# RMS norm with repeated rows: stores and later loads issued by GpSimd in place of SyncE

## The chip, the cores and the metric

The kernel runs on one core of one Trainium2 chip. The metric is the device time of one execution in microseconds (us), the median over several runs. Profiles come from one execution each.

## The reference

```python
def reference(x, gamma):            # x: 8 x 512 x 2048 float32, gamma: 2048 float32
    x_rep = np.repeat(x, 2, axis=1) # each row twice: 8 x 1024 x 2048
    rms = np.sqrt((x_rep ** 2).mean(axis=-1, keepdims=True) + 1e-6)
    x_norm = x_rep / rms
    return (x_norm * gamma[None, None, :]).astype(np.float32)
```

Each of the 4096 rows is divided by its root mean square, multiplied by gamma, and written twice. The input has 33.6 MB, the output 67.1 MB.

## The kernel before

The 4096 rows are handled in four loads of 1024 rows. A load (`load`, L49) brings 8 rows of 2048 floats to each of 128 partitions, 64 KB in a partition, 8.39 MB in all. Each load gives two stores (`store`, L52) of the same size, since every row goes out twice; a store takes 8 finished rows (4 rows, each repeated) of each partition. So there are four loads and eight stores, twelve transfers of 8.39 MB. The 64 KB of a partition are one contiguous run in memory and in the buffer.

All rows live in one buffer `y` of 24 rows per partition, seen as three regions of 8 rows: `first`, `second` and `third`. Function `four` handles two loads, `n` and `m`, and is called twice, for loads 0 and 1 and then for loads 3 and 2. Load `n` goes to the last half of `first` and the first half of `second` (`first + K`), load `m` to `third`. From there:

- `squares` (ACT, L63 and L67) sums the squares of each row and takes the root.
- `scale` (DVE, L76 and L77) takes the reciprocal and multiplies the row by it and by gamma, into the place where the first copy of the row stands in the output.
- `repeat` (L84) copies each finished row to the place beside it, on ACT in five of the seven calls of one `four`, on DVE in two (one in each half of load `n`).
- `store` sends a region out.

The order is written out by hand (`manual_schedule`): each engine runs its instructions in the order of the program text, and the semaphores are put in by the framework. The stores of one `four` are, in order: `n`'s first half out of `first`, `n`'s second half out of `second`, `m`'s first half out of `first`, `m`'s second half out of `third`. The region `first` is written again (L77) when its earlier store has landed. The loads of the second `four` wait for stores of the first: load 3 overwrites parts of `first` and `second`, so it waits for the first three stores; load 2 overwrites `third` and waits for the fourth.

Before the change all twelve transfers are issued by SyncE, so they stand in one queue in the order load, load, four stores, load, load, four stores. Gamma is loaded by four small transfers issued by ACT, ahead of the second load in the program text, and spread over the partitions by two GpSimd instructions (L133, L137).

Of the kernel before, what the change touches and what calls it, by code (L numbers as in the profile page):

```python
# [1 line left out]

# [4 lines left out]


@with_exitstack
def kernel(  # L10
    ctx: ExitStack,
    tc: tile.TileContext,
    x: bass.AP,
    gamma: bass.AP,
    out: bass.AP,
):
    nc = tc.nc
    P = nc.NUM_PARTITIONS
    f32 = mybir.dt.float32
    Act = mybir.ActivationFunctionType  # L20
    Alu = mybir.AluOpType

    B, S, D = x.shape
    Bo, So, Do = out.shape
    R = So // S
    assert R == 2 and D == Do and B == Bo and So == S * R
    eps = 1e-6
    inv_d = 1.0 / float(D)


    K = 4
    N = B * S
    ntiles = N // (P * K)
    assert N % (P * K) == 0 and ntiles == 8
    H = 2
    x_t = x.rearrange("b s d -> (b s) d").rearrange("(n p k) d -> n p k d", p=P, k=H * K)
    out_t = out.rearrange("b s d -> (b s) d").rearrange("(n p h j) d -> n h p (j d)", p=P, h=H, j=K * R)

    singles = ctx.enter_context(tc.tile_pool(name="singles", bufs=1))
    rows = ctx.enter_context(tc.tile_pool(name="rows", bufs=1))  # L40
    junk = ctx.enter_context(tc.tile_pool(name="junk", bufs=1, space=bass.MemoryType.PSUM))
    small = ctx.enter_context(tc.tile_pool(name="small", bufs=4))

    y = rows.tile([P, 3 * K * R, D], f32, name="y")
    first, second, third = 0, K * R, 2 * K * R

    def load(n, at):  # L49
        nc.sync.dma_start(out=y[:, at : at + H * K, :], in_=x_t[n])  # L50

    def store(n, h, to):  # L52
        nc.sync.dma_start(
            out=out_t[n, h], in_=y[:, to : to + K * R, :].rearrange("p j d -> p (j d)")
        )

    def squares(at, rows):

        n = len(rows)
        ss = small.tile([P, n], f32, name=f"ss{n}")  # L60
        for c, k in enumerate(rows):
            sq = junk.tile([P, D], f32, name="sq")
            nc.scalar.activation(  # L63
                out=sq[:], in_=y[:, at + k, :], func=Act.Square, accum_out=ss[:, c : c + 1]
            )
        rms = small.tile([P, n], f32, name=f"rms{n}")
        nc.scalar.activation(out=rms[:], in_=ss[:], func=Act.Sqrt, scale=inv_d, bias=eps_t[:])  # L67
        return rms

    def scale(at, to, rows, rms, at_once=K):  # L70
        n = len(rows)
        rstd = small.tile([P, n], f32, name=f"rstd{n}")
        for c, k in enumerate(rows):
            if c % at_once == 0:
                part = slice(c, min(c + at_once, n))
                nc.vector.reciprocal(out=rstd[:, part], in_=rms[:, part])  # L76
            nc.vector.scalar_tensor_tensor(  # L77
                out=y[:, to + R * k, :], in0=y[:, at + k, :], scalar=rstd[:, c : c + 1],
                in1=gamma_b[:], op0=Alu.mult, op1=Alu.mult,
            )  # L80

    def repeat(to, k0, k1, copy):
        y_r = y[:, to + R * k0 : to + R * k1, :].rearrange("p (k r) d -> p k r d", r=R)
        copy(out=y_r[:, :, 1, :], in_=y_r[:, :, 0, :])  # L84

    ctx.enter_context(tc.manual_schedule())

    half = K // 2
    up, down = list(range(K)), list(range(K - 1, -1, -1))

    def four(n, m, constants, at_once):


        load(n, first + K)
        constants()
        load(m, third)
        for rows, n_at_once in ((up[:half], half), (up[half:], at_once)):
            scale(first + K, first, rows, squares(first + K, rows), n_at_once)
        repeat(first, 0, half, nc.scalar.copy)
        repeat(first, half, K, nc.vector.tensor_copy)  # L100
        store(n, 0, first)
        scale(second, second, down, squares(second, down))
        repeat(second, half, K, nc.scalar.copy)
        repeat(second, 0, half, nc.vector.tensor_copy)
        store(n, 1, second)
        roots = [squares(third + h * K, up) for h in range(H)]
        scale(third, first, up, roots[0])
        repeat(first, 0, half, nc.scalar.copy)
        repeat(first, half, K, nc.scalar.copy)
        store(m, 0, first)  # L110
        scale(third + K, third, up, roots[1])
        repeat(third, 0, K, nc.scalar.copy)
        store(m, 1, third)

    gamma_b = singles.tile([P, D], f32, name="gamma_b")
    G, E = 16, 3
    C = D // G - E
    gamma_s = y[0:1, 0:2, :].rearrange("p k (c d) -> p (k c) d", c=G // 2)
    gamma_t = y[0:1, 2, :]
    eps_t = singles.tile([P, 1], f32, name="eps_t")  # L120

    def constants():
        nc.scalar.dma_start(
            out=gamma_s[0:1, :, :C],
            in_=gamma[: G * C].rearrange("(p c d) -> p c d", p=1, c=G),
        )
        for c in range(E):
            at = G * C + c * G
            nc.scalar.dma_start(
                out=gamma_t[0:1, c * G : (c + 1) * G],  # L130
                in_=gamma[at : at + G].partition_broadcast(1),
            )
        nc.gpsimd.partition_broadcast(  # L133
            out_ap=gamma_b[:, : G * C].rearrange("p (c d) -> p c d", c=G),
            in_ap=gamma_s[0:1, :, :C],
        )
        nc.gpsimd.partition_broadcast(out_ap=gamma_b[:, G * C :], in_ap=gamma_t[0:1, : E * G])  # L137
        nc.vector.memset(eps_t, eps)  # L138

        root = singles.tile([P, 1], f32, name="root")[:]  # L140
        nc.scalar.activation(out=root, in_=eps_t[:], func=Act.Sqrt)  # L141

    four(0, 1, constants, 1)
    four(3, 2, lambda: None, half)


# [1 line left out]
_INS = ['x', 'gamma']  # L148
_OUTS = [((8, 1024, 2048), 'float32')]


# [23 lines left out]
```

## Time and profile before

| what | value |
|---|---|
| median of 3 runs | 238.1 us (238.0 to 238.66) |
| span of the profiled execution | 236.3 us (its own time is not listed beside the span) |
| DMA engines, share of the span, big transfers | 98.7% |
| mean rate | 426 GB/s |
| ACT busy | 110.2 us (47%) |
| DVE busy | 84.5 us (36%) |
| GpSimd (POOL) busy | 2.8 us (1%) |
| median time from issue to landing | loads 31.4 us, stores 24.9 us |

The span goes from the first to the last instruction of the program. The share of the DMA engines is the time that packets took on the core's 16 DMA engines, divided by 16 spans. The chain that ended last is the sequence of work and transfers, followed back from the end, in which each piece released the next one. The time from issue to landing of a transfer includes the time that it stood in its queue behind others.

### The profile page before, as it was taken

The page shows a single profiled execution, that of the slowest core. Times are in us where ns is not written, and L with a number is a line of the kernel's source. Part 1 is how long each engine was busy: PE and PEld are TensorE (multiplying, and loading weights), DVE is VectorE, ACT ScalarE, POOL GpSimd, SP SyncE. Part 2 cuts the span into 40 slices and gives each one's busy share as a digit, 9 for nine tenths or more (in the row PEclk, how much of TensorE's full clock was granted, in tenths as well). Part 3 has the DMA queues.
Part 4 walks back from the last instruction along what each step waited for, and adds up shares of the span by engine and source line. Part 5 has one row for each costly group of instructions (what it writes and reads, how often), then busy time and mean ns, then how long its engine had stood idle before and what let it go on. Part 6 is the DMA issues. An engine that isn't in the chain of part 4 may idle for free.

```text
span 236.3 us, 226 instructions
## 1 busy us (share of the span) xinstructions
DVE 84.5 (36%) x48; ACT 110.2 (47%) x86; POOL 2.8 (1%) x6
## 2 busy tenths in 40 slices
DVE  0000496594699500000000007928919992000000
ACT  2001989479998470000000049991999957400000
POOL 0110000000000000000000000000000000000000
DMA  9898989989898989989898998989898988989894
GB/s 355 356 533 355 521 366 477 411 366 521 355 533 356 499 388 466 422 366 521 355 533 355 488 399 355 533 355 533 355 533 355 499 388 377 510 355 533 355 533 178
DMA packets 1767, 100.68 MB, mean 426 GB/s; under 512 B 230, under 2 KB 230, under 8 KB 230
## 3 DMA queue, kind: packets, MB, share of 16 engines
q1 hardware_dynamic: 1728, 100.66, 98.7%
q10 hardware_dynamic: 38, 0.01, 0.0%
q14 instruction: 1, 0.01, 0.0%
HBM read 33.56 MB, written 67.11 MB: 426 GB/s over the span
## 4 chain that ended last, share of the span: by engine, by line
DMA 45%; ACT 26%; DVE 12%; issue 2%; DVEq 0%
DMA y<-in_x_dram 26%; DMA out_dram<-y 20%; ACT sq L63 15%; DVE y L77 12%; ACT y L84 11%; ACT rms L67 1%; DVE rstd L76 0%; DVEq L77 0%
## 5 line engine op out<-in xcount | busy, mean ns | idle before, releaser
L63 ACT ACTIVATE sq<-y 128x2048 f32<-128x2048 f32 x32 | 60.1, 1878 | 71.1 <-DMA y<-in_x_dram 70.4
L77 DVE SCALAR_TENSOR_TENSOR y<-y,rstd,gamma_b 128x2048 f32<-128x2048 f32 x32 | 73.8, 2349 | 1.6 <-DMA out_dram<-y 1.0
L84 ACT COPY y<-y 128x4096 f32<-128x4096 f32 (+1 forms) x10 | 42.6, 4284 | 19.1 <-DVE y L77 18.3
L76 DVE RECIPROCAL rstd<-rms 128x4 f32<-128x4 f32 (+2 forms) x11 | 1.9, 169 | 109.2 <-ACT rms L67 109.2
L84 DVE COPY y<-y 128x4096 f32<-128x4096 f32 x4 | 9.2, 2294 | 0.1
L63 ACT ACTIVATION_READ_ACCUMULATOR sq<-y 128x1 f32 x32 | 6.0, 186 | 0.0
L67 ACT ACTIVATE rms<-ss,eps_t 128x4 f32<-128x4 f32 (+1 forms) x10 | 3.0, 297 | 0.3
L141 ACT ACT_TABLE_LOAD x1 | 1.3, 1283 | 2.6 <-issue 2.6
L133 POOL PARTITION_BROADCAST gamma_b<-y x1 | 2.2, 2243 | 10.2 <-DMA y<-in_gamma_dram 10.2
L137 POOL PARTITION_BROADCAST gamma_b<-y x1 | 0.3, 323 | 10.1 <-DMA y<-in_gamma_dram 10.1
L138 DVE MEMSET eps_t<- 128x1 f32 x1 | 0.1, 59 | 0.8 <-PEq L159 0.8
L141 ACT ACTIVATE root<-eps_t 128x1 f32<-128x1 f32 x1 | 0.2, 203 | 0.0
L159 POOL MEMSET const-uint8-127<- 128x1 uint8 x1 | 0.1, 102 | 0.0
L159 POOL MEMSET const-bfloat16-1.0<- 128x1 bf16 x1 | 0.1, 101 | 0.0
L159 POOL MEMSET const-float32-0.0<- 128x1 f32 x1 | 0.1, 98 | 0.2 <-issue 0.2
L159 POOL MEMSET const-float32-1.0<- 128x1 f32 x1 | 0.1, 98 | 0.0
## 6 DMA issues: line engine op xcount, KB each, us to landing
out_dram<-y SPq DMA_DIRECT2D x8, 24.9
y<-in_x_dram SPq DMA_DIRECT2D x4, 31.4
y<-in_gamma_dram ACTq DMA_DIRECT2D x3, 0.1 KB
y<-in_gamma_dram ACTq DMA_DIRECT2D x1, 7.8 KB, 9.9
```

The source lines that it names most:

```text
L63: nc.scalar.activation(out=sq[:], in_=y[:, at + k, :], func=Act.Square, accum_out=ss[:, c : c + 1])
L67: nc.scalar.activation(out=rms[:], in_=ss[:], func=Act.Sqrt, scale=inv_d, bias=eps_t[:])
L76: nc.vector.reciprocal(out=rstd[:, part], in_=rms[:, part])
L77: nc.vector.scalar_tensor_tensor(out=y[:, to + R * k, :], in0=y[:, at + k, :], scalar=rstd[:, c : c + 1], in1=gamma_b[:], op0=Alu.mult, op ...
L84: copy(out=y_r[:, :, 1, :], in_=y_r[:, :, 0, :])
L133: nc.gpsimd.partition_broadcast(out_ap=gamma_b[:, : G * C].rearrange("p (c d) -> p c d", c=G), in_ap=gamma_s[0:1, :, :C],)
L137: nc.gpsimd.partition_broadcast(out_ap=gamma_b[:, G * C :], in_ap=gamma_t[0:1, : E * G])
L138: nc.vector.memset(eps_t, eps)
L141: nc.scalar.activation(out=root, in_=eps_t[:], func=Act.Sqrt)
L159: nc = _bacc.Bacc("TRN2", target_bir_lowering=False, num_devices=1)
```

## The change

The loads take the issuing engine as an argument: the first call of `four` issues its two loads from SyncE, the second call from GpSimd. All eight stores are issued by GpSimd. The order of the program text, the buffer, the compute instructions and the waits for data are the same.

```diff
-    def load(n, at):
-        nc.sync.dma_start(out=y[:, at : at + H * K, :], in_=x_t[n])
+    def load(n, at, by):
+        by.dma_start(out=y[:, at : at + H * K, :], in_=x_t[n])
 
     def store(n, h, to):
-        nc.sync.dma_start(
+        nc.gpsimd.dma_start(
             out=out_t[n, h], in_=y[:, to : to + K * R, :].rearrange("p j d -> p (j d)")
         )
...
-    def four(n, m, constants, at_once):
+    def four(n, m, constants, at_once, by):
 
-        load(n, first + K)
+        load(n, first + K, by)
         constants()
-        load(m, third)
+        load(m, third, by)
...
-    four(0, 1, constants, 1)
-    four(3, 2, lambda: None, half)
+    four(0, 1, constants, 1, nc.sync)
+    four(3, 2, lambda: None, half, nc.gpsimd)
```

In the built program GpSimd's two broadcasts stand ahead of its ten transfers (four stores, two loads, four stores), and SyncE is left with two loads and the waits at the end of the program (L170).

## The prediction

> **What bounds the kernel now.** I read the queue part of the page first, then its 40 slices, then the chain of waits, then the timeline of the issuing engine.
>
> Queues (queue and kind: packets, MB, share of the 16 DMA engines' span) and the busy row of the DMA engines in tenths:
>
> ```profile
> DMA  9898989989898989989898998989898988989894
> q1 hardware_dynamic: 1728, 100.66, 98.7%
> ```
>
> All twelve big transfers, four loads and eight stores of 8.39 MB, run on one queue, and its packets fill 98.7% of what 16 engines have in the span of 236.3 us. The idle rest is 1.3%, 3.1 us. The busiest compute engine, ACT, has 110.2 us. So the kernel is bound by its DMA engines, in every stage, and the question is whether they stay as full and their packets as fast.
>
> The chain that ended last (start us, us, what), cut to its DMA pieces:
>
> ```profile
> 0.72 21.93 DMA y<-in_x_dram
> ...
> 76.17 23.92 DMA out_dram<-y
> ...
> 100.11 38.74 DMA y<-in_x_dram
> ...
> 155.33 22.23 DMA out_dram<-y
> ```
>
> The reader should take the ends: 22.65, 100.09, 138.85 and 177.55 us. Between them lie 4, 2 and 2 transfers, so one takes 77.44/4 = 19.36, 38.76/2 = 19.38 and 38.70/2 = 19.35 us. The packet records give the reason: a transfer is 128 packets of 65,536 B, 8 on each of 16 engines, and a packet takes 2.418 us at the median and at the least; 8 x 2.418 = 19.34. One transfer follows another without a gap. The landings that the trace records are at 22.65, 42.05, 61.39, 80.80, 100.09, 119.60, 138.85, 158.21, 177.55, 196.85, 216.15 and 235.44 us: eleven steps of 19.34 in the mean. What is not this pace is 3.3 us before the first landing (22.65 - 19.34) and 0.8 after the last one.
>
> Then the issues (start us, us, engine line op). They show why there is no gap:
>
> ```profile
> 39.27 48.17 SPq L53 DMA_DIRECT2D out_dram<-y  x4
> 100.11 19.85 SPq L50 DMA_DIRECT2D y<-in_x_dram  x2
> 155.33 48.29 SPq L53 DMA_DIRECT2D out_dram<-y  x4
> ```
>
> Every transfer is issued while an earlier one is still moving. One at a time, the issues are at 39.27, 55.89, 76.17, 87.11 (four stores), 100.11, 119.62 (two loads), 155.33, 171.98, 192.26 and 203.28 (four stores). I subtract each from the landing of the transfer ahead of it, and this is the lead: 2.78, 5.50, 4.63, 12.98, 19.49, 19.23, 2.88, 5.57, 4.59 and 12.87 us. The least are 2.78 and 2.88, at the first store of each half.
>
> **The change part by part.** The profiled execution is told by its span alone, 236.3 us; the median of the runs is 238.1, so I put 1.8 us around the span and add my terms to the span.
>
> *Ten issues leave SyncE.* An issue costs 0.33 to 0.35 us there, and all of it lies in the leads above: nothing is won.
>
> *Ten issues go to GpSimd, in the same order with the same waits.* GpSimd's own work is 2.8 us, and its last piece (L137, 0.32 us) ends at 23.3 us, 16 us ahead of the first store. What queues behind a waiting issue is the next transfer, exactly as on SyncE. What a plain transfer costs GpSimd to issue, the trace of before does not show. Nearest rows: from below SyncE's 0.33 us; from above GpSimd's longest instruction, the broadcast of 2.24 us at L133. Both are under the smallest lead of 2.78 us, so this term is 0. Should it be longer, the excess shows at those two first; at 5 us it would be 2.2 + 2.1 + 0.4 + 0.4 = 5.1 us over the four short leads, since 4.63 and 4.59 are then short too.
>
> The Trainium skill (page "DMA: Bandwidth & Descriptors", section "Specifications") gives about 1 us to the first byte for GpSimd's path and about 0.6 us for the one used now; by that the term is an extra 0.4 us per issue, also inside every lead, and the sum stays.
>
> *VectorE beside the new issues.* The kernel's VectorE copies move 4096 elements a partition in 2.29 us while its multiplies take 2.35 us for 2048, so the copies run in a mode of twice the rate. They stand here (start us, us, engine line op):
>
> ```profile
> 36.91 2.29 DVE L84 COPY y<-y 128x4096 f32<-128x4096 f32 x1
> 53.52 2.29 DVE L84 COPY y<-y 128x4096 f32<-128x4096 f32 x1
> 152.97 2.29 DVE L84 COPY y<-y 128x4096 f32<-128x4096 f32 x1
> 169.61 2.29 DVE L84 COPY y<-y 128x4096 f32<-128x4096 f32 x1
> ```
>
> Each ends 0.07 to 0.1 us before the store that reads it is issued (39.20 to 39.27, 55.81 to 55.89), because that store waits for it; after it VectorE is idle until 44.01, 60.85, 160.10 and 176.94. No other issue stands beside a copy. Two stores (76.17, 192.26) stand beside multiplies that end at 80.03 and 196.21; if those blocked GpSimd to their end, 3.9 us, the leads of 4.63 and 4.59 would still hold, with 0.7 us to spare. I book 0, and 0 to 1 us for the bounds.
> The Trainium skill speaks against the change here (page "SBUF — State Buffer", section "SBUF: two separate sides"): while VectorE runs such a fast mode, GpSimd can't write the descriptors of its transfers, and the transfer waits. By that rule a store would be late by what is left of a copy, and here nothing of a copy is left, so the sum by rule and by row is the same; a copy moved behind the issue would cost up to 2.29 us against a lead of 2.78.
>
> *Another queue.* So far loads and stores stand in one queue, in order. With GpSimd's queue the first store (39.27) can share the engines with the end of the second load, which has 2.78 us left, about one packet on each engine. At worst the load lands a packet later, 42.05 + 2.42 = 44.5 us; its first reader is the squares at 52.38 (L63), 7.9 us away. The engines do the same work in another order: 0.
>
> *The packets of GpSimd's queue.* Ten of twelve transfers, 10 x 19.34 = 193.4 us of the span, now depend on the size and speed of packets that no row of before shows. Below there is nothing to win: 2.418 us is the least that any packet of 64 KB took, and the steps between landings are already 8 of them. Above: the gamma loads have packets of 500 B in 25 to 27 ns, where 2.418 us per 64 KB would make 18 ns, so a packet costs some 8 ns of its own. Pieces of 8 KB in place of 64 KB would add 7 x 8 = 56 ns to 2418 (2.3%, 4.5 us on 193.4); of 4 KB 120 ns (5%, 9.6 us). The access patterns are the same 64 KB runs per partition on both sides, so I take whole packets, and 0; both ends stay for the range.
>
> *Junctions on GpSimd's queue.* Nine times a GpSimd transfer follows another. Nearest rows: 0.00 us on SyncE's queue (19.34 against 8 x 2.418), and the start of the first load, 21.93 - 19.34 = 2.6 us. I take 0.04 each, close to SyncE's, since the successor is queued 2.8 to 19 us ahead: 0.3 us in all, bounds 0 and 9 x 2.6 = 23 us.
>
> *The end.* SyncE still waits for all landings at L170, and after the last one there are 0.8 us in the profile. GpSimd's drain there is 34 ns; with transfers of its own to clear up it may take longer. I take 0.2 us, bounds 0 and 1.
>
> Sum: 236.3 + 0 + 0.3 + 0.2 = 236.8 in the span, 238.6 with the 1.8 around it.
>
> **The rivals.** A run of this kernel against itself tells about 0.3%, 0.7 us: 237.4 to 238.8 is "the same".
>
> *Slower packets (slower).* GpSimd's queue cuts the runs into smaller pieces or some engines serve it more slowly, and since every transfer lands with its slowest engine, each per cent costs 1.9 us. It decides from 0.4% on. For it: the kernel has no idle DMA time to take it up. Against: same runs, same engines. With 8 KB pieces 238.6 + 4.5 = 243.1, with 4 KB 248.2; chance 0.27. The Trainium skill has such a rule (page "DMA: Bandwidth & Descriptors", section "Latency and other measured facts"): engines 7 and 15 are usually the slower ones, by its best guess because of GpSimd's descriptor rings; in before nothing of it shows, as the median packet is the fastest one.
>
> *Gaps at the junctions (slower).* The queue on GpSimd does not run ahead: each successor starts some time after its forerunner. For it: no trace here shows two GpSimd transfers in a row. Against: the leads. 0.5 us each make 238.6 + 4.2 = 242.8; it decides from 0.1 us each. Chance 0.13.
>
> *A longer end or first issue.* 0.5 to 1.5 us more, 239.1 to 240.1; chance 0.06.
>
> *Faster.* Two queues would have to keep the engines fuller than one. For it: 1.3% of their time is idle. Against: nearly all of that lies ahead of the first landing and behind the last one, where both kernels do the same. A gain over 0.7 us needs packets under 2.41 us; 1% less is 236.7. Chance 0.08.
>
> That the issues do not move is not a rival: the built program has ten on GpSimd and two on SyncE.
>
> **How the numbers follow.** The forecast, no measurable change, has 0.46; slower 0.27 + 0.13 + 0.06 = 0.46; faster 0.08. The likeliest single case gives 238.6, with its own range 237.6 to 239.4. The whole range goes from 237.6 to 246.0: it leaves out the gain (0.08), most of the 4 KB case (0.07) and the dear junctions (0.05), 0.2 in all.
>
> **What would show it.** Right: two queues in part 3, one with 16.8 MB and one with 83.9 MB and still 64 KB packets, together about 98%; landings of transfers 19.3 to 19.4 us apart; the second load at most 2.4 us later. Wrong: more packets than 1536 + the small ones or a share over 99% in a longer span (slower packets); a step over 19.5 us between landings with a lower digit in the DMA row at each (gaps); a hole at 42 or 158 us alone (issue cost over 2.8 us); a span as before with a longer time around it (the end).

## The result and the profile after

The changed kernel takes 240.36 us (240.01 to 240.81, 4 runs) against 238.11 (238.0 to 238.66, 4 runs): 1.0081 times as long, 95% interval 1.0059 to 1.0103 (the two medians alone make 1.0094). The profiled execution took 240.18 us with a span of 238.3, so 1.9 us lie around the span as before (1.8), and the 2.0 us in the span (238.3 - 236.3) are the loss.

Queues (queue and kind: packets, MB, share of the 16 engines' span) and DMA row of the changed kernel:

```profile
DMA  9898989899898989899999998989898989999894
q0 software_dynamic: 1440, 83.89, 81.9%
q1 hardware_dynamic: 288, 16.78, 16.5%
```

GpSimd's ten transfers have 144 packet records each, as SyncE's had (1728 / 12): eight of 64 KB and one of 4 B for each engine. The pieces did not get smaller. The shares sum to 98.4% (98.7% before).

The chain's DMA pieces (start us, us, what), and GpSimd's issues from the timeline (start us, us, engine line op):

```profile
0.73 21.95 DMA y<-in_x_dram
...
76.44 24.89 DMA out_dram<-y
...
101.95 38.34 DMA y<-in_x_dram
```

```profile
39.83 0.68 POOL L53 DMA_DIRECT2D out_dram<-y  x1 [16.47 <-ACT sq L63]
56.40 0.54 POOL L53 DMA_DIRECT2D out_dram<-y  x1 [15.89 <-DVE y L84]
76.44 0.53 POOL L53 DMA_DIRECT2D out_dram<-y  x1 [19.50 <-ACT y L84]
88.67 0.53 POOL L53 DMA_DIRECT2D out_dram<-y  x1 [11.70 <-ACT y L84]
```

The chain's ends are 22.68, 101.33 and 140.29 us, where before had 22.65, 100.09 and 138.85. So the loss is there by the end of the third store: 1.2 us of the 2.0. The issues of the first two stores stand 0.56 and 0.51 us later than SyncE's did, and each takes 0.53 to 0.68 us in place of 0.34.

Who waits for the first store shows its landing: VectorE may overwrite `first` only then (start us, us, instruction, idle before it and its releaser). The first line is of before, the second of the changed kernel:

```profile
61.51 4.61 DVE L77 SCALAR_TENSOR_TENSOR y<-y,rstd,gamma_b 128x2048 f32<-128x2048 f32 x2 [0.48 <-DMA out_dram<-y]
```

```profile
62.80 2.35 DVE L77 SCALAR_TENSOR_TENSOR y<-y,rstd,gamma_b 128x2048 f32<-128x2048 f32 x1 [1.77 <-DMA out_dram<-y]
```

It starts 1.29 us later. The landings that the trace records are 22.68, 42.02, 62.72, 82.03, 101.34, 120.64, 140.29, 159.63, 178.95, 198.28, 217.75 and 237.12 us. Their steps from the second landing on are 20.70, 19.31, 19.31, 19.30, 19.65, 19.34, 19.32, 19.33, 19.47 and 19.37. The step to the first store is 1.36 above the pace of 19.34; the nine after it are 0.34 above it in sum; and from the last landing to the end of the span there are 1.21 us in place of 0.83. That makes 1.36 + 0.34 + 0.38 = 2.08 us, the whole loss. Counted by landings, two thirds of it belong to one place, the first store, and the experiments are about that.

The packet records show what happened there. The engines end the second load at 40.96 to 41.57 us and begin the store at 41.20 to 41.75: on the mean an engine stands idle for 0.2 us. The store's first packet then takes 2.5 to 2.7 us in place of 2.42 on 15 engines and 3.92 us on one. That one is 1.3 us behind the mean of the others from then on, and a transfer has landed when its last engine has. At the end of the fourth store the others lose as much: their last packet there takes 3.02 to 3.53 us on 15 engines and 2.418 on the one that is behind, and from then on all end within 0.4 to 0.7 us of each other. So the landings tell what the slowest engine lost; taking the one packet of 3.92 us away need not give 1.36 us back.

### The profile page after: what moved, and what is told of

The parts are those of the page before. It is cut to its first block, busy times and chain, and to the rows that moved or that the text cites. A ratio compares the mean times of both kernels' runs of the same rounds, so it can differ in the third digit from the quotient of the medians.

```text
span 238.3 us, 227 instructions
## 1 busy us (share of the span) xinstructions
DVE 84.5 (35%) x48; ACT 110.2 (46%) x86; POOL 8.2 (3%) x16
## 4 chain that ended last, share of the span: by engine, by line
DMA 36%; issue 23%; ACT 14%; DVE 13%; POOL 1%; POOLq 0%; DVEq 0%
DMA y<-in_x_dram 25%; DVE y L77 11%; DMA out_dram<-y 10%; ACT sq L63 10%; ACT y L84 3%; DVE y L84 2%; POOL out_dram L53 1%; ACT rms L67 1%; DVE rstd L76 0%; POOLq L170 0%; POOLq L53 0%; POOLq L50 0%; DVEq L77 0%
## 5 line engine op out<-in xcount | busy, mean ns | idle before, releaser
L53 POOL DMA_DIRECT2D out_dram<-y x8 | 4.4, 552 | 145.4 <-ACT y L84 61.2
L50 POOL DMA_DIRECT2D y<-in_x_dram x2 | 1.1, 532 | 31.2 <-DMA out_dram<-y 31.2
```

Source lines behind the costliest of these rows:

```text
L50: by.dma_start(out=y[:, at : at + H * K, :], in_=x_t[n])
L53: nc.gpsimd.dma_start(out=out_t[n, h], in_=y[:, to : to + K * R, :].rearrange("p j d -> p (j d)"))
```

## The experiments

The times of before beside each group of runs were 238.19 to 238.3 us. "Stretch" is the time that the packets of a transfer take over 2.418 us, summed and divided by 16 engines; nearly all of it lies in one packet of each engine. (The records do not name the engine; 16 rows of packets follow from each packet beginning where another ends.) Where a copy on VectorE is left out or done in place (e1_early, e5_mid, e6_early_sync, e10_mid_sync, e12_copy_onto_itself), one or two rows of the first store are written as they were loaded, so these kernels serve for the times alone. "First step" is the first store's landing less the first load's, and it is too long by what it has over two paces of 19.34.

**e1_early**: the first GpSimd store is ready 2.3 us earlier.

```diff
-        repeat(first, half, K, nc.vector.tensor_copy)
+        if n != 0:
+            repeat(first, half, K, nc.vector.tensor_copy)
```

> The changed kernel with VectorE's copy of two rows in the first half of the first call of four left out, so that the first store writes two unscaled rows in each partition. The store is then ready about 2.3 us earlier (at about 36.9 in place of 39.2 us). Theory late issue: the first GpSimd store costs 1.3 us only because its packets come after the engines have run dry; with the lead it starts without a hole, its landing falls from 62.7 to about 61.4 us and the kernel takes about 239.0 us. Theory first use (the first transfer that GpSimd issues stalls one engine, whenever it comes) and theory change of queue (each passing from SyncE's to GpSimd's queue costs about 1.3 us): landing stays near 62.7 us, time 240.3 us.

Measured: 239.79 us, ratio 1.0064 (1.0052 to 1.0076). The store was issued at 37.58 us and no engine stood idle, but the first step is still 0.78 too long: now the last packet of the load ahead took 3.0 to 3.6 us on all engines (stretch 0.89), and this load landed at 45.33 us. A lead does not cure the loss: less is lost, and it lies in the load. That landing is 3.28 us later than before, about a packet of the store (2.42) and the stretch (0.89): the load's 64 KB packets end by 42.54 us, but on four engines its last record, of 4 B, follows the store's first packet, at 44.54 to 44.95 us.

**e2_late_sync**: on SyncE alone, the first store is issued at 40.59 us.

```diff
         repeat(first, half, K, nc.vector.tensor_copy)
+        if n == 0:
+            repeat(first, K - 1, K, nc.vector.tensor_copy)
```

> The kernel before, all on SyncE, with one row copied once more on VectorE ahead of the first store, 1.15 us, so that this store is issued at about 40.4 in place of 39.3 us. Theory late issue: its packets come at about 41.4 us, as late as in the changed kernel, the engines run dry at 41.0 to 41.7 us, and the kernel loses 0.3 to 1.3 us: 238.4 to 239.4 us, with a landing of the first store at 61.7 to 62.7 us. Theories first use and change of queue: nothing of GpSimd is in it, 238.1 us.

Measured: 240.07 us, 1.0071 (1.0059 to 1.0083), more than any theory gave. But the place is another one. VectorE's wait for the first store:

```profile
61.79 2.35 DVE L77 SCALAR_TENSOR_TENSOR y<-y,rstd,gamma_b 128x2048 f32<-128x2048 f32 x1 [0.71 <-DMA out_dram<-y]
```

The hole itself, with packets from 41.44 us on, costs the first step only 0.27 us. The rest comes later: the fourth store's last packets are stretched by 0.80, and the load behind it lands at 140.80 us, 1.95 later than in before. So a late store on SyncE is as dear in the sum as the change, and yet not the same thing.

**e3_all_gpsimd**: one queue, GpSimd's, for all twelve.

```diff
-        constants()
         load(m, third, by)
+        constants()
...
-    four(0, 1, constants, 1, nc.sync)
+    four(0, 1, constants, 1, nc.gpsimd)
```

> The changed kernel with the first two loads on GpSimd too, both ahead of the gamma broadcasts: one queue, twelve transfers. Theory late issue: the first store is as late as in the changed kernel and costs the same, 240.3 us, plus what the first load's later start on GpSimd costs, up to 1 us. Theory change of queue: no passing is left, the first store lands at most 19.4 us behind the second load, 239.0 us plus that start. Theory first use: the stall moves to the first load, which lands at about 24 in place of 22.7 us, and the first store costs nothing.

Measured: 241.46 us, 1.0126 (1.0109 to 1.0143). The first load lands at 23.40 us, 0.75 later than in before. The first store, issued at 40.52 us and again too late to find busy engines, has a first step only 0.29 too long. VectorE's wait for that store:

```profile
62.51 2.35 DVE L77 SCALAR_TENSOR_TENSOR y<-y,rstd,gamma_b 128x2048 f32<-128x2048 f32 x1 [0.74 <-DMA out_dram<-y]
```

No passing of queues, no loss of 1.3 us there; what remains is the hole of e2_late_sync, and as there the fourth store's packets are stretched (0.84). In the sum nothing was won: this is the slowest kernel of all (the profiled execution, at 240.75 us, was the fastest of four). The time is that of the theory of late issue, 240.3 and up to 1 us, and not the 239.75 of the theory of the change of queue; but the loss does not lie at the first store, where late issue had it.

**e4_warm**: a small GpSimd load at the start.

```diff
+    warm = singles.tile([P, 16], f32, name="warm")
+    nc.gpsimd.dma_start(out=warm[:], in_=x_t[0][:, 0, :16])
     four(0, 1, constants, 1, nc.sync)
```

> The changed kernel with one small load of 64 B in each partition issued by GpSimd at the start of the program. Theory first use: the stall is paid there, hidden beside the first load, and the first store lands at about 61.4 us, 239.0 us in all. Theories late issue and change of queue: nothing changes, 240.3 us.

Measured: 240.12 us, 1.0074 (1.006 to 1.0088); first step 1.20 too long, again with one packet of 3.93 us. That GpSimd had not yet issued a transfer is not the cause.

**e5_mid**: the GpSimd store ready 1.15 us earlier.

```diff
-        repeat(first, half, K, nc.vector.tensor_copy)
+        repeat(first, half if n else K - 1, K, nc.vector.tensor_copy)
```

> The changed kernel with VectorE copying one row in place of two in the first half of the first call of four (one row of the first store is left as it was loaded). The first store is ready about 1.15 us earlier; its packets should come at about 40.1 us, after the second load's last packets have begun (38.5 to 39.2) and before the first engine runs dry (41.0), as on SyncE before. Theory late issue: no hole, first landing of a store at 61.4 to 61.7 us, 238.7 to 239.0 us in all (what is left is the end and small things). Theory two queues at once (a store that comes while the other queue's load is moving stretches that load's last packets by 0.9 us, as seen in e1_early): landing at 62.2, 239.6 us or more.

Measured: 239.97 us, 1.0068 (1.0054 to 1.0081). The first store:

```profile
38.72 0.68 POOL L53 DMA_DIRECT2D out_dram<-y  x1 [15.57 <-issue]
```

```profile
62.84 2.35 DVE L77 SCALAR_TENSOR_TENSOR y<-y,rstd,gamma_b 128x2048 f32<-128x2048 f32 x1 [1.85 <-DMA out_dram<-y]
```

Issued early enough that every engine passes from load to store without a hole (41.07 to 41.77), it lands as late as in the changed kernel. On all 16 engines its first packet takes 3.6 to 4.0 us (stretch 1.35). Here the theory that lateness is the cause fell. The other theory expected the stretch in the load's last packets, and they have 0.12 only; it is in the store's first packet.

**e6_early_sync**: as e1_early, on SyncE's one queue.

```diff
-        repeat(first, half, K, nc.vector.tensor_copy)
+        if n != 0:
+            repeat(first, half, K, nc.vector.tensor_copy)
```

> The kernel before, all on SyncE, with VectorE's copy of two rows in the first half of the first call of four left out (these rows of the first store are written as they were loaded), so the first store is issued 2.3 us earlier on the one queue. Theory two queues at once: nothing of it can happen on one queue, the second load lands at 42.0 and the first store at 61.4 us, 238.1 to 238.3 us. Theory early store (a store that is queued so early disturbs the load's end on any queue): the load's last packets take 3.3 us as in e1_early and the time is about 239.2 us.

Measured: 239.46 us, 1.0047 (1.0034 to 1.006). The rival was right: issued at 36.81 us, the store disturbs the load's end on one queue too (stretch 1.36, first step 1.55 too long). The issue and VectorE's wait for the store:

```profile
36.81 0.35 SPq L53 DMA_DIRECT2D out_dram<-y  x1
```

```profile
62.88 2.35 DVE L77 SCALAR_TENSOR_TENSOR y<-y,rstd,gamma_b 128x2048 f32<-128x2048 f32 x1 [2.01 <-DMA out_dram<-y]
```

GpSimd is not needed for a loss of this size.

**e7_last_store**: only the last store on GpSimd, behind a store on SyncE.

```diff
-        nc.sync.dma_start(
+        by = nc.gpsimd if (n, h) == (2, 1) else nc.sync
+        by.dma_start(
```

> The kernel before with the last store alone issued by GpSimd, 12 us ahead of the end of the store before it, which is moving on SyncE's queue. Theory of the end (GpSimd's drain costs 0.3 to 0.4 us behind the last landing): 1.2 us from the last landing to the end of the span in place of 0.8, 238.6 us. Theory two queues at once: besides that some packets are stretched when the second queue joins at about 204 us, 0.9 us more, 239.5 us.

Measured: 238.49 us, 1.0009 (0.9994 to 1.0024). The two stores share the engines from 210 us on, landing at 224.10 and 236.17, and no packet of either is stretched (0.01 and 0.00). Two queues at once, store beside store, cost nothing. From the last landing to the end there are 0.93 us, so one GpSimd transfer makes 0.1 us of the end, less than expected.

**e8_before_again**: the kernel before, unchanged.

> The kernel before, unchanged, for a second profile on another chip: does the stretch of the fourth store's last packets ahead of the first load of the second half (0.2 us in the first profile of before, 0.8 to 0.9 in the changed kernel, e2_late_sync, e3_all_gpsimd and e4_warm) belong to the late first store, or does it come and go by itself? Theory late issue: 0.2 us again, landings as in the first profile, 238.1 to 238.5 us. Rival: 0.8 us here as well.

Measured: 238.03 us in one run, the landings within 0.1 us of the first profile, the fourth store's stretch 0.22 again (0.19 in the first profile). It belongs to the kernel before, and the 0.8 to 0.9 to the kernels with a late first store.

**e9_touch**: a small store to the output and a small load of far rows at the start, by GpSimd.

```diff
+    touch = singles.tile([P, 32], f32, name="touch")
+    nc.vector.memset(touch[:, :16], 0.0)
+    nc.gpsimd.dma_start(out=out_t[0, 0][:, :16], in_=touch[:, :16])
+    nc.gpsimd.dma_start(out=touch[:, 16:], in_=x_t[3][:, 0, :16])
     four(0, 1, constants, 1, nc.sync)
```

> The changed kernel with two small transfers issued by GpSimd at the start: a store of 64 B from each partition to the place of the output that the first store overwrites later, and a load of 64 B per partition from the input rows that the second half loads first. Theory first touch (the first write to the output, on each DMA engine, costs up to 1.4 us once, and the first read of the far input rows up to 0.9 us; in before they happen to be covered): both are paid at the start, the packets of the first store and those at the end of the fourth store are back at 2.42 us, the loss is the end and at most 0.3 us for the hole, 238.7 to 239.0 us. Theory moment of the first store (the loss depends on when the store's packets reach the engines at the end of the second load): nothing changes, 240.1 us.

Measured: 240.19 us, 1.0067 (1.0044 to 1.009). The first step is 1.30 too long, with 14 of the 16 first packets of the store at 3.5 to 4.0 us (stretch 1.16). As far as 64 B in each partition can show it, the first touch of these addresses is not the cause.

**e10_mid_sync**: as e5_mid, on SyncE's one queue.

```diff
-        repeat(first, half, K, nc.vector.tensor_copy)
+        repeat(first, half if n else K - 1, K, nc.vector.tensor_copy)
```

> The kernel before, all on SyncE, with VectorE copying one row in place of two in the first half of the first call (one row of the first store is left as it was loaded), so that the first store is issued at about 38.1 us, between e6_early_sync (36.8 us, 239.46 us) and before (39.3 us, 238.2 us). Theory moment of the first store: packets reach the engines at about 39.0 us, as in e1_early, and the time is between the two, 238.6 to 239.5 us. Rival, left-out work (what costs in e6_early_sync, e1_early and e5_mid is that VectorE leaves a copy out, not the moment): half of the copy left out, half of the loss, 238.8 us, with the stretch spread evenly. Rival, noise: 238.2 us.

Measured: 238.89 us, 1.0022 (1.0007 to 1.0037). Issued at 38.05 us; the load's last packets are stretched by 0.96. As the moment theory had it, the loss lies between e6_early_sync and before. The rival of left-out work gave nearly the same, 238.8 us, so this run does not tell the two apart.

**e11_last_four**: the last four stores on GpSimd, the rest on SyncE.

```diff
-        nc.sync.dma_start(
+        by = nc.gpsimd if n in (3, 2) else nc.sync
+        by.dma_start(
```

> The kernel before with the last four stores alone issued by GpSimd: the loads and the first four stores stay on SyncE. The first of the four has the same short lead as the first store of the kernel (it is issued some 2 us before the engines run dry, again from SyncE's load to GpSimd's store). Theory moment of the first store (what costs is the first meeting of loads and stores near 41 us, not GpSimd): nothing is stretched at 157 us, the first half is as in before, and what is left is the end, 0.35 us, and at most 0.2 us in slower packets: 238.5 to 238.8 us. Rival, each late GpSimd issue behind a load costs 1.3 us: 239.9 us.

Measured: 239.76 us, 1.0061 (1.0049 to 1.0074): the rival's value. The issue of the first of the four, VectorE's waits for the first store of each half (the line numbers are one higher here), and a piece of the chain:

```profile
155.82 0.68 POOL L54 DMA_DIRECT2D out_dram<-y  x1 [132.56 <-ACT sq L64]
```

```profile
61.51 4.61 DVE L78 SCALAR_TENSOR_TENSOR y<-y,rstd,gamma_b 128x2048 f32<-128x2048 f32 x2 [0.58 <-DMA out_dram<-y]
```

```profile
178.96 2.35 DVE L78 SCALAR_TENSOR_TENSOR y<-y,rstd,gamma_b 128x2048 f32<-128x2048 f32 x1 [1.91 <-DMA out_dram<-y]
```

```profile
100.09 38.70 DMA y<-in_x_dram
```

The first half is that of before: the wait at 61.51 us, the load at 138.79. In the second half the first GpSimd store stands behind a SyncE load, and the same loss comes in a new place: the step from 158.12 to 178.88 us is 20.76, 1.42 too long. The engines stood idle for 0.01 us on the mean: the packets begin at 157.24 to 157.79 us as the load's end there, and take up to 3.99 us (stretch 1.22). In the changed kernel the same pair of transfers, both on GpSimd's queue, takes 159.63 to 178.95: 19.32. This is the cleanest pair of all: the same store by the same engine, issued 1.42 and 1.34 us before the first DMA engine runs out of the load, and only the queue of the load differs.

**e12_copy_onto_itself**: the control for the copies that were left out.

```diff
-        repeat(first, half, K, nc.vector.tensor_copy)
+        if n != 0:
+            repeat(first, half, K, nc.vector.tensor_copy)
+        else:
+            same = y[:, first + R * half : first + R * K, :].rearrange("p (k r) d -> p k r d", r=R)[:, :, 0, :]
+            nc.vector.tensor_copy(out=same, in_=same)
```

> The kernel before, all on SyncE, with VectorE's copy in the first half of the first call writing the two rows onto themselves in place of the rows beside them: the same time on VectorE, so the first store is issued at about 39.3 us as in before, but its two rows are left as they were loaded, as in e6_early_sync. Theory moment of the first store: 238.2 us, no packet stretched near 41 us. Rival, left-out work or unscaled rows in the store are what costs in e6_early_sync: 239.4 us.

Measured: 238.32 us, 1.0002 (0.9993 to 1.0012). The content of the rows does not matter. What is left for e6_early_sync and e10_mid_sync is the moment; that VectorE is idle there in place of copying was not changed without changing the moment.

**What the runs show together.** The first place of the loss is where a DMA engine passes from a load to a store. The table has the first store of each kernel (its first half); for the two second halves the last column counts from the landing of the load ahead. The column of the fourth store belongs to the first half.

| kernel | load, store issued by | store issued at, us | stretch of the load's packets, of the store's | stretch of the fourth store's | step too long by |
|---|---|---|---|---|---|
| before | SyncE, SyncE | 39.27 | 0.03, 0.00 | 0.19 | 0.05 |
| e10_mid_sync | SyncE, SyncE | 38.05 | 0.96, 0.00 | 0.00 | 1.07 |
| e6_early_sync | SyncE, SyncE | 36.81 | 1.36, 0.00 | 0.00 | 1.55 |
| e2_late_sync | SyncE, SyncE | 40.59 | 0.01, 0.10 | 0.80 | 0.27 |
| changed kernel | SyncE, GpSimd | 39.83 | 0.01, 0.26 | 0.88 | 1.35 |
| e4_warm | SyncE, GpSimd | 39.80 | 0.00, 0.26 | 0.77 | 1.20 |
| e9_touch | SyncE, GpSimd | 39.94 | 0.03, 1.16 | 0.19 | 1.30 |
| e5_mid | SyncE, GpSimd | 38.72 | 0.12, 1.35 | 0.00 | 1.44 |
| e1_early | SyncE, GpSimd | 37.58 | 0.89, 0.00 | 0.01 | 0.78 |
| e11_last_four, second half | SyncE, GpSimd | 155.82 | 0.00, 1.22 | - | 1.42 |
| e3_all_gpsimd | GpSimd, GpSimd | 40.52 | 0.06, 0.13 | 0.84 | 0.29 |
| changed kernel, second half | GpSimd, GpSimd | 157.26 | 0.00, 0.07 | - | none |

From a SyncE load to a GpSimd store the loss was there in all six rows (0.8 to 1.4 us). On SyncE's queue alone it was there only when the store was issued more than a microsecond earlier than in before. That the change of queue is what costs is shown by e11_last_four against the changed kernel's second half (that GpSimd issues its first transfer there is not the reason, by e4_warm). A second pair agrees, e5_mid against before, if the way from the issue to the first packet is counted as 1.37 us on GpSimd (changed kernel) and 0.85 us on SyncE (e2_late_sync): by this estimate the stores reach the engines at the same moment, 40.09 and 40.12 us, and the steps are too long by 1.44 and 0.05. The row of e1_early does not show it: its store and that of e10_mid_sync reach the engines at 38.95 and 38.90 us, and both stretch the load alike, by 0.89 and 0.96.

Engine by engine the records show one thing more. In the changed kernel the engine with the packet of 3.92 us has no stretch at the end of the fourth store, and the 15 others have 0.60 to 1.11 us there; e4_warm is the same (0 on one, 0.49 to 1.06 on 15). In e1_early, e5_mid, e6_early_sync and e10_mid_sync, where every engine was stretched at the first store or the load ahead of it, no engine has more than 0.12 at the fourth. In e9_touch the two engines with the shortest first packets (2.64 and 2.95 us) have the most at the fourth (0.85 and 1.11). In e2_late_sync and e3_all_gpsimd, where no engine had more than 0.11 at the first place, every engine has 0.43 to 1.11. So in these kernels an engine loses its microsecond at one of the two places, and e3_all_gpsimd, with one queue for all, only lost it later. Not settled: what in the DMA engines stretches these packets, why the fourth store is the second place, and why before pays so little at either.

## Why the prediction was right and where it was wrong

The time lies in the range (237.6 to 246.0), but not in the likeliest case: "no measurable change" with 238.6 had 0.46, and the kernel is slower by 0.81%, beyond the 0.3%. Slower had the same chance. None of the rivals names the mechanism; "a longer end or first issue", with 0.06, names two of the three places and was too small at 239.1 to 240.1. The likeliest case's own range (237.6 to 239.4) was missed by 1 us. That the whole range holds the time is luck in part: its upper end was set for smaller packets and for gaps at every junction, and neither came. Of the signs named for being wrong, the hole came, at 41.2 us, but with an issue of 0.68 us and not of over 2.8.

- *What bounds the kernel*: held. Sixteen full engines, 19.3 us for each transfer, and no engine makes up for what it lost.
- *Packets of GpSimd's queue, taken as whole and 0*: held. The packets have 64 KB, and half of them take 2.418 to 2.422 us. Slower packets, the dearest rival, did not come. The Trainium skill's slow engines 7 and 15 (page "DMA: Bandwidth & Descriptors", section "Latency and other measured facts") do not show: the median packet on GpSimd's queue takes 2.422 us against 2.418 on SyncE's in before, and after the fourth store no engine is more than 0.7 us behind another.
- *Issue on GpSimd, booked at 0*: here the first step failed. The leads were counted to the landing of the transfer ahead, 42.05 us. The engines have moved its last bytes 0.4 to 1.1 us before that, at 40.99 to 41.68. So the lead of the first store was 1.7 us, not 2.78. And the issue on GpSimd costs more than its 0.53 to 0.68 us: from the end of the last copy (39.22) to the issue 0.6, from there to the first packet 1.37, 2.0 in all; SyncE took 0.06 and 0.85 in e2_late_sync. This made the hole of 0.2 us. The Trainium skill's 1 us and 0.6 us to the first byte (page "DMA: Bandwidth & Descriptors", section "Specifications") have the order right, and both are short of the 1.37 and 0.85 us measured here.
- *Another queue, booked at 0*: here the sum failed. The text saw that load and store would meet on two queues and gave the engines the same work in another order. What it left out is the stretch where a SyncE load hands over to a GpSimd store: the term is 1.2 to 1.4 us, not 0 (1.42 in e11_last_four, with no hole). It also left out that the fourth store can be stretched in its place. The load's later landing was right in kind: in e1_early it landed at 45.33, where the text allowed 44.5; the packet that it allowed was there, and the stretch came on top.
- *VectorE's copies*: no store met one, as worked out.
- *Junctions, 0.3 us*: measured 0.34 over nine steps. *The end, 0.2 us*: measured 0.38. GpSimd's drain is over 0.46 us after the last landing, and SyncE's own waits 0.24 after it.

With the handover at 1.36 the sum would have been 236.27 + 1.36 + 0.34 + 0.38 = 238.35 in the span, against 238.33 measured.

## What to carry to other kernels

When DMA engines are full all the time, moving an issue costs nothing only if the successor stays queued: count its lead from the moment when the engines run out of packets, not from the landing that a semaphore reports, and take the whole way from the last wait to the first packet as the price. A plain transfer moves as fast from GpSimd's queue as from SyncE's, but passing from a load on SyncE's queue to a store on GpSimd's cost 1.2 to 1.4 us in five kernels here. One queue is no cure by itself: with all twelve transfers on GpSimd's queue the kernel was slowest, as the stretch came in the fourth store. Only SyncE's queue with the first store issued as in before had little at either place, so look at every handover, packet by packet. And an early issue is not always better: the same store, a microsecond earlier on its own queue, made the kernel slower.

## What the runs showed of the hardware

- A store queued behind a load early enough stretches the load's last packet on every engine, from 2.42 to 3.1 to 4.1 us, even on one queue (e6_early_sync, e10_mid_sync); behind another store, where e7_last_store has the second queue join, it does not.
- An engine that is behind does not catch up, since each engine has its own 8 packets of every transfer: in the changed kernel one packet of 3.92 us on one of 16 engines sets the landings of the first three stores, until the 15 others lose as much in the fourth.
- The landing of a transfer comes 0.4 to 1.1 us after its engines have run out of its packets (before: 40.99 to 41.68, landing at 42.05); with a store behind it on another queue, it came a packet later still (45.33 in e1_early).
- From the end of the last wait to the issue GpSimd takes 0.56 to 0.61 us at the first, second, fifth and sixth store and at the first load, and 0.3 at the other five; SyncE 0.02 to 0.07.
